# A one-core encoder block: Fourier parts prepared in the attention, a sum made by the fetching DMA, and a merge in program order

## The chip, the cores and the metric

The kernel runs on one core of a Trainium2 chip. The metric is the device time of one execution in microseconds (us). The kernel before took 1730.04 us (median of 3 runs, 1729.23 to 1732.54).

## The reference, cut to what matters

One encoder layer is run on two sequences, 256 and 1024 positions, each with 16 meta tokens ahead, at width 1024, all in float32:

```python
h = rms_norm(x, norm_mix_g)
z = h @ w_in          # q | k | v | f | attention gate | Fourier gate
a  = bidirectional_gqa(q, k, v) @ w_attn_o       # 8 query heads, 2 kv heads of 64
fo = fourier_mix(f) @ w_four_o                   # real part of a 2-D DFT, 4 groups of 128
merged = sigmoid(z_attn) * a + sigmoid(z_four) * fo
x = x + merged @ w_out
u = rms_norm(x, norm_ffn_g) @ w_ffn_in
x = x + (silu(gate) * up) @ w_ffn_out            # d_ff 2816, then a final rms_norm
```

## The kernel before, in words

Every float32 product is made of float32r parts. An operand is cast on ScalarE to a high part, and the rest is subtracted into a low part on VectorE or GpSimd (`split`, line 204). TensorE then adds three products, high by high, high by low and low by high (`three`, lines 224 to 226). Tokens are cut into chunks 0 and 1 (512 sample tokens each) and 2 (256 prompt tokens).

SBUF is a set of 48 slots of 128 x 1056 elements (27 single ones, 7 triples), handed out in the order in which they came free (`Slots`). Whoever gets a slot waits, on the chip, until its former users are through with it.

The stages, in order: norm and Fourier input (`stage_a`); the DFT (`fourier`), whose result goes folded to DRAM as `f_d`, 516 rows by 656 columns; `q_pass` and `kv_pass`; the attention; the merge; `w_out`; the two feed-forward products. The gate logits (`gate_gen`) are 16 units of 128 rows. Each is a product for each chunk, stored to DRAM (`gates`). They fill gaps of TensorE: in the attention the loop calls `gates(FILL[kind])` after every step, and the filler issues product groups until their costs (640 for a group of three 512-column matmuls, 320 for 256 columns) have used up what was added.

The attention takes ten tiles of 128 queries, the two prompt tiles first, each in two groups of four heads. A head is a score product (L891) into the one score buffer, a maximum (L896), an exponential (L903), and a scaling. A second part follows one group later: transposes (L825), a cast and a subtraction (L827, L828), and products with the values (L845, L846). The last group's second part is the drain. The result of a group is written to DRAM, twice: as both value parts' products, `a_d[c][0]` and `a_d[c][1]`, whose sum is the attention's output.

Inside a `manual_schedule` block TensorE, ScalarE and VectorE execute in the order in which the program names their work. Outside, and for SyncE and GpSimd always, a planner orders each engine's instructions by dependencies and estimated times, so a load can be issued well ahead of its place in the program. Each engine works off its own queue in order. The attention is such a block; the merge is not.

After the attention, `fourier_parts` (line 931) fetches `f_d` and splits it into six slots, and the row of channel 64 with its weights into small zero-padded tiles (L947 to L968). `load_af(c)` (line 972) fetches both halves of a chunk of `a_d` (L987), adds them on VectorE (L998) and splits the sum. Chunk 0 is done beside the remaining gates, chunks 2 and 1 after them.

`merge` (line 1003) runs eight steps, one for each 128 rows of the output. `load(i)` fetches three weight pieces (L1015 to L1018) and six gate pieces (L1024) on SyncE's queue. `need(i)` prepares the weights `wf` (Fourier) and `wm` (attention) (L1032 to L1037). `sigmoid(i)` is one activation for each chunk over both gates (L1046). `fourier(i)` makes the Fourier product in four PSUM banks, unfolds it (L1070 to L1078) and multiplies it by its gate on GpSimd (L1087). Then follow the attention products of chunks 0, 2 and 1, each with a gate product (L1125), a sum on GpSimd (L1126), and the rounding of the merged rows into two parts (L1128, L1129). `fourier(i + 1)` is named ahead of step i's attention products. Last, `w_out` loads its weights with `need` (line 1146), a unit ahead of use.

## Time and profile before

| | us |
|---|---|
| median of 3 runs | 1730.04 (1729.23 to 1732.54) |
| the profiled execution: its own time | 1730.22 |
| its span, first to last instruction | 1728.5 |
| TensorE busy in the span | 1679.2 |
| VectorE, ScalarE, GpSimd busy | 1115.0, 720.5, 272.6 |

The times in the views are microseconds from the span's start. PE is TensorE's matmul, PEld its weight load, DVE VectorE, ACT ScalarE, POOL GpSimd, SP SyncE, and SPq its queue of transfers. A number behind L is a line of the kernel. An idle time is put down to what ended it (the releaser); where a wait was for several things, to the last. The granted clock is the share of TensorE's full speed in that stretch.

### The profile page before, as it was taken

The numbers are of one execution on the slowest core, as the hardware profiler recorded it, in microseconds if no ns is written. First come the engines' busy times: TensorE is split into PE (matmuls) and PEld (weight loads), VectorE is DVE, ScalarE is ACT, GpSimd is POOL, SyncE is SP. The second block draws the span as 40 slices with busy tenths as digits, with TensorE's granted clock in tenths as the row PEclk, the third lists the DMA queues.
The fourth block names the chain that finished last, engine by engine and source line by source line (L and its number), as shares of the span: only waits on it lengthen the run. The fifth ranks groups of instructions, "written<-read, shape, count | busy, mean of one in ns | idle before, by whom it ended". The sixth has DMA issues, their size and how long they took to land.

```text
span 1728.5 us, 25882 instructions
## 1 busy us (share of the span) xinstructions
PE 1679.2 (97%) x9837; PEld 1499.2 (87%) x9837; DVE 1115.0 (65%) x2082; ACT 720.5 (42%) x1411; POOL 272.6 (16%) x307
## 2 busy tenths in 40 slices
PE   7999999999999998989989999999999999999997
PEld 7888879878888886878879999999999998888886
DVE  5423544567777775752479676667666768765685
ACT  6323323456666665631355222222222234444444
POOL 3002333210100113663353000000000000000002
PEclk9999999999999998999999999999999999999999
DMA  5144331322212228624442222322232137653534
GB/s 191 57 147 138 116 116 56 122 74 67 70 57 64 62 66 291 212 92 154 162 155 82 87 68 91 102 91 83 95 103 90 65 123 259 199 186 95 162 97 153
DMA packets 97564, 203.03 MB, mean 117 GB/s; under 512 B 10173, under 2 KB 46169, under 8 KB 97440
## 3 DMA queue, kind: packets, MB, share of 16 engines
q1 hardware_dynamic: 88224, 184.22, 32.5%
q10 hardware_dynamic: 7824, 12.53, 2.0%
q0 software_dynamic: 1392, 4.63, 0.9%
q8 instruction: 77, 1.26, 0.3%
q14 instruction: 47, 0.39, 0.1%
HBM read 143.30 MB, written 58.04 MB: 116 GB/s over the span
## 4 chain that ended last, share of the span: by engine, by line
PE 88%; DVE 5%; issue 2%; ACT 2%; POOL 2%; DMA 1%; SPq 0%; POOLq 0%; ACTq 0%; DVEq 0%
PE i L224 10%; PE i L226 10%; PE i L225 10%; PE o L226 5%; PE o L225 5%; PE o L224 5%; PE g L224 4%; PE pt L825 4%; PE g L226 4%; PE S L891 4%; PE g L225 4%; PE pv L845 2%; PE pv L846 2%; PE wo L226 2%; PE wo L225 2%
## 5 line engine op out<-in xcount | busy, mean ns | idle before, releaser
L1320 ACT CAST w<-wi 128x512 fp32r<-128x512 f32 x168 | 104.0, 621 | 273.2 <-PE i L226 223.9
L224 PE MATMUL i<-A,w 128*128 128x384 f32 x616 | 208.6, 339 | 3.0 <-ACT w L1320 2.6
L226 PE MATMUL i<-A,w 128*128 128x384 f32 x616 | 208.3, 339 | 2.4 <-POOL w L1322 2.4
L225 PE MATMUL i<-A,w 128*128 128x384 f32 x616 | 208.1, 338 | 0.0
L226 PE MATMUL i<-Ah,w 128*128 128x256 f32 x616 | 173.3, 282 | 0.0
L224 PE MATMUL i<-Ah,w 128*128 128x256 f32 x616 | 173.1, 281 | 0.2 <-ACT w L1320 0.2
L225 PE MATMUL i<-Al,w 128*128 128x256 f32 x616 | 173.1, 281 | 0.0
L828 DVE TENSOR_TENSOR pT<-pt,pT 128x512 fp32r<-128x512 f32 x156 | 106.9, 686 | 37.9 <-ACT pT L827 36.7
L827 ACT CAST pT<-pt 128x512 fp32r<-128x512 f32 x156 | 90.8, 582 | 95.0 <-PE pt L825 92.1
L1322 DVE TENSOR_TENSOR w<-wi,w 128x512 fp32r<-128x512 f32 x154 | 105.1, 684 | 29.1 <-ACT w L1320 28.6
L233 POOL TENSOR_SCALAR fin0r<-fin0ss 128x1 f32<-128x1 f32 x1 | 0.8, 788 | 755.3 <-ACT X L241 755.3
L224 PEld LDWEIGHTS i<-A,w 128*128 128x128 f32 x616 | 116.5, 189 | 3.5 <-ACT w L1320 2.8
L896 DVE TENSOR_REDUCE sm<-S 128x1 f32<-128x1040 f32 (+1 forms) x80 | 86.5, 1081 | 50.7 <-PE S L891 47.4
L226 PEld LDWEIGHTS i<-A,w 128*128 128x128 f32 x616 | 116.4, 189 | 3.2 <-POOL w L1322 3.2
L224 PEld LDWEIGHTS i<-Ah,w 128*128 128x128 f32 x616 | 116.1, 188 | 0.6 <-ACT w L1320 0.6
L225 PEld LDWEIGHTS i<-A,w 128*128 128x128 f32 x616 | 116.3, 189 | 0.0
L225 PEld LDWEIGHTS i<-Al,w 128*128 128x128 f32 x616 | 116.3, 189 | 0.0
L226 PEld LDWEIGHTS i<-Ah,w 128*128 128x128 f32 x616 | 116.1, 189 | 0.0
L903 ACT ACTIVATE p<-S,sm 128x1040 f32<-128x1040 f32 (+1 forms) x80 | 80.3, 1003 | 33.7 <-DVE sm L896 27.1
L825 PE MATMUL pt<-ident,p 128*128 128x128 f32 (+1 forms) x624 | 93.4, 272 | 0.0
L226 PE MATMUL o<-wfo,act 128*128 128x512 f32 (+1 forms) x212 | 82.1, 388 | 2.0 <-DVE act L1454 2.0
L225 PE MATMUL o<-wfo,act 128*128 128x512 f32 (+1 forms) x212 | 82.0, 387 | 0.0
(747 smaller groups left out, 4438.4 us busy)
## 6 DMA issues: line engine op xcount, KB each, us to landing
wi<-w_fi SPq DMA_DIRECT2D x48, 512.0 KB, 3.5
wg<-w_g SPq DMA_DIRECT2D x32, 512.0 KB, 3.6
act_d<-sc SPq DMA_DIRECT2D x77, 192.0 KB, 1.9
act<-act_d SPq DMA_DIRECT2D x37, 320.0 KB, 4.1
wfo<-w_fo SPq DMA_DIRECT2D x21, 512.0 KB, 4.1
X<-act_d SPq DMA_DIRECT2D x31, 320.0 KB, 3.4
act_d<-sc SPq DMA_DIRECT2D x77, 128.0 KB, 2.3
gate<-gs ACTq DMA_DIRECT2D x32, 256.0 KB, 3.2
```

The source lines that it names most:

```text
L224: mm(out, sh, mh, start=first and i == 0, stop=False)
L225: mm(out, sh, ml, start=False, stop=False)
L226: mm(out, slo, mh, start=False, stop=last and i == n - 1)
L825: nc.tensor.transpose(pt[:rows, h * P : (h + 1) * P], me.ps4[h][:, col : col + rows], self.ident[:])
L827: nc.scalar.copy(pT[:rows, :512], pt[:rows, :])
L828: nc.vector.tensor_tensor(pT[:rows, 512:1024], pt[:rows, :], f32(pT[:rows, :512]), op=ALU.subtract)
L845: nc.tensor.matmul(me.pv[:], vst, pT[:rows, :512], start=j == 0, stop=False)
L891: nc.tensor.matmul(S[:, base + lo : base + hi], hq, self.kT[seq][g][v][:, lo:hi], start=v == 0, stop=v == 1)
L896: nc.vector.tensor_reduce(nb, S[:, base : base + L], axis=AX.X, op=ALU.max, negate=True)
L903: self.last_exp = nc.scalar.activation(p, S[:, base : base + L], AF.Exp, bias=nb, accum_out=total)
L1320: nc.scalar.copy(w[:, :512], src)
L1322: eng.tensor_tensor(w[:, 512:1024], src, f32(w[:, :512]), op=ALU.subtract)
```

## The change

- `fourier_parts` is now stepped inside the attention, once after each head from the loop's step 101 on (tile 4 of the sample), 21 steps in all. Its slots are taken one by one. The subtractions are on GpSimd instead of VectorE. Two slots of prompt keys are given back when the prompt tiles are done.
- `load_af` fetches the first half of a on SyncE's queue and the second on GpSimd's queue with an accumulating DMA into the same tile. The VectorE addition is gone. Chunks 0 and 2 are asked for at the drain's start, chunk 1 after the attention; chunk 0 is split beside the gates, chunk 2 behind them, chunk 1 behind Fourier unit 1 in the merge.
- The filler gets 610 instead of 640 for each step of the sample's attention, and 2600 at five places after it.
- The merge is a manual block. `load` and `load_gates` are two functions. Weights of step i + 3 are asked for, and those of step i + 2 prepared, after step i's first attention product; the gates of step i + 3 after step i, those of step 7 in step 5. `sigmoid` is one activation for each chunk and gate. The rounding of merged rows is put off by one product (`late`).
- `w_out`'s first weight unit is loaded at one call and split at the next.

```diff
+PARTS = 100
...
-    FILL = {"s": 640, "p": 400, "end": 640, "drain": 900}
+    FILL = {"s": 610, "p": 400, "end": 640, "drain": 900}
...
                 sl.put(q.pop(t))
+                if t == 9:
+                    sl.put(*self.kv_slots[4:6])
                 if t == tiles[-1]:
-                    sl.put(*self.kv_slots[:6])
+                    sl.put(*self.kv_slots[:4])
...
+        slots = self.fparts = {}
+
+        def block(i):
+            if i // 3 not in slots:
+                slots[i // 3] = sl.get("fx", F32R, "t")
+            return slots[i // 3][:, i % 3 * HL : (i % 3 + 1) * HL]
+
+        self.fblock = block
+        block(17)
+        y = self.y64 = sl.get("y64", F32R, "t")
+        tails = [(slots[5][:, HL : 3 * HL], self.f_d[512:516, :], NL, 32), (y[:, :D], a["w_64"], D, 64)]
+        raw = [sl.get("x64r") for _ in tails]
+        for r, (t, src, n, _) in zip(raw, tails):
+            nc.gpsimd.memset(f32(t[:68, :]), 0.0)
             for b in (0, 32, 64):
...
-        self.fblock = lambda i: slots[i // 3][:, i % 3 * HL : (i % 3 + 1) * HL]
+        yield 1
+        yield 1
+        for r, (t, _, n, lo) in zip(raw, tails):
+            for b in (0, 32, 64):
+                nc.scalar.copy(t[b : b + 4, :], r[b : b + 4, :n])
+            x = slice(lo, lo + 4)
+            nc.gpsimd.tensor_tensor(t[x, :], r[x, :n], f32(t[x, :]), op=ALU.subtract)
+            sl.put(r)
+            yield 1
         for k in range(4):
-            r = raw.pop(k)
+            r = sl.get("fr")
+            nc.sync.dma_start(r[:, :NL], self.f_d[k * P : (k + 1) * P, :])
+            yield 1
+            yield 1
             for half in range(2):
                 src = r[:, half * HL : (half + 1) * HL]
-                h, l = self.fblock(4 * k + 2 * half), self.fblock(4 * k + 2 * half + 1)
+                h, l = block(4 * k + 2 * half), block(4 * k + 2 * half + 1)
                 nc.scalar.copy(h, src)
-                nc.vector.tensor_tensor(l, src, f32(h), op=ALU.subtract)
+                nc.gpsimd.tensor_tensor(l, src, f32(h), op=ALU.subtract)
+                yield 1
             sl.put(r)
...
         def load(i):
-            if i == len(pieces):
-                return
-            srcs, j = pieces[i]
-            loaded[i] = [sl.get("af") for _ in srcs]
-            for src, raw in zip(srcs, loaded[i]):
-                nc.sync.dma_start(
...
+            if i < 4 // per:
+                raws[i] = sl.get("af")
+                for x, queue in enumerate((nc.sync, nc.gpsimd)):
+                    src = self.a_d[c][x][i * per * P : (i + 1) * per * P, :].rearrange("(k p) n -> p k n", p=P)
+                    queue.dma_start(raws[i].v(per, n), src, **({"accum_op": ALU.add} if x else {}))
 
         load(0)
+        load(1)
         yield 1
-        for i in range(len(pieces)):
-            load(i + 1)
-            raws = loaded.pop(i)
-            if len(raws) == 2:
-                r, x = (r[:, :1024] for r in raws)
-                nc.vector.tensor_tensor(r, r, x, op=ALU.add)
-            out.append(self.split(raws[0], 1024, "af", nc.vector, "t"))
-            sl.put(*raws)
+        for i in range(4 // per):
+            raw = raws.pop(i)
+            out.append(self.split(raw, 1024, "af", nc.vector, "t"))
+            sl.put(raw)
...
             r = sl.get("wmf")
             nc.sync.dma_start(r[:, :512], a["w_mf"][i])
@@ -1017,6 +1015,10 @@
             q = sl.get("wma")
             nc.sync.dma_start(q[:, :512], a["w_ma"][i])
             raws[i] = r, q
+
+        def load_gates(i):
+            if i >= 8:
+                return
             g = gts[i] = [sl.get("gt") for _ in range(3)]
...
+        def sigmoid(i, which):
             for c in range(3):
-                g = gts[i][c][:, : 2 * CH_N[c]]
+                n = CH_N[c]
+                g = gts[i][c][:, which * n : (which + 1) * n]
                 with self.tc.issue_after(self.last_exp.ins):
                     nc.scalar.activation(g, g, AF.Sigmoid)
...
             w = wf.pop(i)
+            sigmoid(i, 0)
             for half in range(2):
...
                     pp.append(pm)
+                while late:
+                    late.popleft()()
                 st = sl.get("fst")
                 nc.scalar.copy(st[:, :HL], pp[0][:, :HL])
...
         load(0)
+        load_gates(0)
         yield 0
         need(0)
         load(1)
+        load_gates(1)
         for c in range(3):
             self.M[c] = [], []
-        sigmoid(0)
+        yield 0
+        need(1)
+        load(2)
+        load_gates(2)
         yield from fourier(0)
-        need(1)
-        sigmoid(1)
-        load(2)
         for i in range(8):
             yield from fourier(i + 1)
+            if i == 0:
+                run_all(self.last_af)
+            if i == 5:
+                load_gates(7)
             if i == 6:
-                sl.put(*self.fparts, self.y64)
+                sl.put(*self.fparts.values(), self.y64)
             if i == 7:
                 next(then)
+            sigmoid(i, 1)
...
                     mv = tuple(af[c][k // per][x][:, (k % per) * n : (k % per + 1) * n] for x in range(2))
                     self.three(pm[:, :n], [(wk, mv)], k == 0, k == 3)
                     yield 3 * n / 2.4
+                if c == 0:
+                    need(i + 2)
+                    load(i + 3)
                 v = gt[:, n : 2 * n]
                 nc.vector.tensor_tensor(v, pm[:, :n], v, op=ALU.mult)
                 nc.gpsimd.tensor_tensor(v, v, gt[:, :n], op=ALU.add)
-                b = (i % per) * n
-                nc.scalar.copy(mh[-1][:, b : b + n], v)
-                nc.vector.tensor_tensor(ml[-1][:, b : b + n], v, f32(mh[-1][:, b : b + n]), op=ALU.subtract)
-                sl.put(gt)
-                if c == 2 and i < 6:
-                    need(i + 2)
-                    sigmoid(i + 2)
+                while late:
+                    late.popleft()()
+
+                def rows(gt=gt, v=v, b=(i % per) * n, n=n, h=mh[-1], l=ml[-1]):
+
+                    nc.scalar.copy(h[:, b : b + n], v)
+                    nc.vector.tensor_tensor(l[:, b : b + n], v, f32(h[:, b : b + n]), op=ALU.subtract)
+                    sl.put(gt)
+
+                late.append(rows)
+                if c == 2 and i == 7:
+                    next(then)
             sl.put(w)
-            if i < 5:
-                load(i + 3)
+            if i < 4:
+                load_gates(i + 3)
+        while late:
+            late.popleft()()
         for c in range(3):
...
-        need(0)
+        raw = sl.get("wo", F32, "s")
+        nc.sync.dma_start(raw[:, :1024], a["w_out"][0])
+        yield 0
+        units[0] = self.split(raw, 1024, "wo", nc.gpsimd, "s")
+        sl.put(raw)
         yield 0
...
                 if i == 7:
                     next(then)
+                    next(then, None)
...
-                for kind, more, slack in self.attention(ps, [8, 9] + list(range(8)), "S", "pv"):
+                parts = self.fourier_parts()
+                for i, (kind, more, slack) in enumerate(self.attention(ps, [8, 9] + list(range(8)), "S", "pv")):
                     while slack and later:
                         later.popleft()()
+                    if slack and i > PARTS:
+                        next(parts, None)
+                    if kind == "drain" and not self.af:
+                        next(m)
+                        early = chain(self.load_af(0), self.load_af(2))
+                        next(early)
                     gates(self.FILL[kind] + more)
                 while later:
                     later.popleft()()
                 self.later = None
-            early = chain(self.fourier_parts(), self.load_af(0))
-            next(early)
-            next(m)
-            for _ in early:
-                gates(1300)
-            gates.rest()
+                run_all(parts)
+                gates(2600)
+                next(m)
+                self.last_af = self.load_af(1)
+                for i, _ in enumerate(early):
+                    gates(2600)
+                    if i == 0:
+                        next(self.last_af)
+                gates.rest()
             self.free_hT(self.hT[1])
...
-            for c in (2, 1):
-                run_all(self.load_af(c))
...
-            run_all(m)
+            with self.tc.manual_schedule(engines={E.PE, E.Activation, E.DVE}):
+                run_all(m)
```

36 lines of the change are left out of this document (4 added, 32 removed).

## The prediction

> **What bounds the kernel now.** First the page's span and engine shares, then the windows by stage (columns: stretch, its length, busy time of PE, its weight loads, DVE, ACT and POOL, granted clock, DMA share, GB/s).
>
> ```profile
> span 1728.5 us, 25882 instructions
> PE 1679.2 (97%) x9837; PEld 1499.2 (87%) x9837; DVE 1115.0 (65%) x2082; ACT 720.5 (42%) x1411; POOL 272.6 (16%) x307
> ...
> 400.00:640.00 240.00, 240.00 (x1478) 206.03 (x1477) 189.79 (x284) 153.06 (x278) 23.79 (x19) 1.00 0.21 61
> 640.00:659.90 19.90, 19.90 (x119) 16.19 (x117) 10.75 (x18) 14.73 (x25) 5.73 (x5) 1.00 0.57 170
> 659.90:667.70 7.80, 7.80 (x46) 6.87 (x46) 0.00 (x0) 5.38 (x7) 1.87 (x1) 1.00 0.69 173
> 667.70:680.00 12.30, 6.69 (x36) 5.21 (x34) 9.99 (x15) 5.83 (x11) 3.83 (x3) 0.99 1.05 387
> 680.00:693.00 13.00, 9.86 (x26) 6.80 (x27) 10.96 (x13) 4.64 (x7) 7.89 (x7) 0.50 1.03 369
> 693.00:753.10 60.10, 59.49 (x340) 53.88 (x339) 43.15 (x85) 34.12 (x56) 39.51 (x50) 1.00 0.52 176
> 753.10:768.00 14.90, 9.96 (x52) 8.79 (x51) 8.82 (x19) 3.89 (x8) 10.34 (x17) 0.89 0.17 56
> ```
>
> TensorE is busy 97% of the span, so only its own idle and slow time can be won. The attention (to 659.9) and the gates after it leave none. The merge starts at 667.7, and there the idle time is 12.30-6.69 = 5.61, 13.00-9.86 = 3.14, 60.10-59.49 = 0.61 and 14.90-9.96 = 4.94: 14.30 us. The clock adds to it: at 0.50 the 9.86 us of work of 680 to 693 would take 4.93, so 4.93 are lost, and 0.11 x 14.90 = 1.64 in the last window. What the merge can give is 14.30+6.57 = 20.9 us. Next the waits of PE there (total, times, longest), and the timeline of PE at the two long ones and at one whole chunk.
>
> ```profile
> PE fo L224 <- ACT wm L1036: 7.6, 2, 4.5
> PE m L224 <- ACT afh L208: 2.0, 2, 1.5
> PE m L225 <- DVE afh L209: 1.8, 1, 1.8
> ```
> ```profile
> 671.15 0.42 PE L224 MATMUL fo<-fx,wm 128*128 128x328 f32 x1 [3.10 <-ACT wm L1036]
> ...
> 720.65 0.32 PE L1059 MATMUL fo<-fx,y 68*128 68x328 f32 x1
> ...
> 724.54 0.40 PE L224 MATMUL m<-y,ml 128*128 128x512 f32 x1
> ...
> 731.46 0.31 PE L1059 MATMUL fo<-fx,y 68*128 68x328 f32 x1
> ...
> 757.88 0.42 PE L224 MATMUL fo<-fx,wm 128*128 128x328 f32 x1 [4.47 <-ACT wm L1036]
> ```
>
> A Fourier unit takes 724.54-720.65 = 3.9 us of PE, a step with its three attention products 731.46-720.65 = 10.8; the products' 6.9 split by their 512, 256 and 512 columns into 2.76, 1.38 and 2.76. The start (to 693.7) waits for weights, then for the halves of a: 9.36 us idle and 4.93 of clock, 14.3. The second place, 753.1 to 768, waits once more for weights: 4.94 and 1.64, 6.6. Why they are late stands in the chain of waits, in the DMA issues (KB each, median us to landing) and in SyncE's timeline and waits.
>
> ```profile
> 660.89 0.32 SPq L855
> ...
> 664.17 7.98 DMA af<-a_d
> 672.25 1.24 DVE af L998
> ```
> ```profile
> wi<-w_fi SPq DMA_DIRECT2D x48, 512.0 KB, 3.5
> af<-a_d SPq DMA_DIRECT2D x10, 512.0 KB, 6.8
> a_d<-ao SPq DMA_DIRECT2D x36, 128.0 KB, 2.5
> tabc<-pos_c POOLq DMA_DIRECT2D x4, 520.0 KB, 4.9
> ```
> ```profile
> 729.22 13.38 SPq L1024 DMA_DIRECT2D gt<-gate  x10
> 746.99 0.33 SPq L1015 DMA_DIRECT2D wmf<-w_mf  x1
> ```
> ```profile
> SPq L1015 <- DVE wmf L1032: 9.8, 1, 9.8
> ```
>
> At the start ten fetches of a, the last two of the map and three sets of weights and gates ask at once; the DMA engines are full (387 and 369 GB/s), and the five DVE additions follow. At 753 the weights were asked for at 746.99, behind ten gate fetches that took 13.38 us to be issued.
>
> **The change part by part.**
>
> *Second place.* Weights of step 7 are asked for after the first product of step 4, no longer behind gate fetches. The products at 724.54 are step 3's, so that is 724.54+2.76+10.8, some 738, against 746.99; they are split after the first product of step 5, 10.8 us later, and a load of that kind lands in 3.5 to 6.8. By my count of the allocator 44 of 48 slots are then taken, so SyncE need not wait long. Value taken: the whole 6.6 is won; bounds 0 (the old slot wait of 9.8 comes back) and 6.6. The gates of step 7 are now asked for late, in step 5; what is late next is ScalarE's sigmoid of step 6, and PE can run through 3.9+6.9 us of work on its eight PSUM banks before it needs that.
>
> *Start: what goes.* The map's four 128-row pieces and their small rows are prepared in the attention: eight 128x328 casts and eight subtractions leave the start. The five additions leave DVE. Fetches of chunks 0 and 2 of a, and weights and gates of step 0, are asked for in the drain (640 to 659.9, where DMA is at 0.57) and just after. FILL 610 for 640 holds back 120 x 30 = 3,600 of gate work by the program's costs. The 7.80 us from 659.9 hold seven groups costed 640 and eight costed 320, 7,040, so 3,600 are 4.0 us of PE, out of the attention and into the gap. PE time is only moved; but the gates then last 7.8+4.0 = 11.8 us after the attention, and with Fourier unit 0 (3.9, its weights split early) PE has work for 15.7 us.
>
> *Start: what comes.* PE, ACT and DVE now keep program order. The split of chunk 2 of a stands on ACT and DVE ahead of the weights of Fourier unit 1. So unit 1 waits for three accumulating fetches on POOL's queue (two of chunk 1, one of chunk 2), each behind its plain fetch. No trace row shows an accumulating fetch. The last stores of a go out 1.0 us after the attention (660.89), land in 2.5; with their issue about 4.4. Plain fetch: 3.5 (alone) to 6.8 (in the crowd), to 7.9 or 11.2. Accumulate: near bound 4.9, the POOL-queue load of its size, one after the other sharing the engines at 387 GB/s (0.5 MB is 1.4 us): the third lands at 7.9+4.9+1.4 = 14.2 to 11.2+4.9+2.7 = 18.8. Far bound twice 6.8, since it must read and write its target: 11.2+13.6+2.7 = 27.5. Then the split and the weights:
>
> ```profile
> 673.51 1.05 ACT L208 CAST y<-af 128x1024 fp32r<-128x1024 f32 x1 [0.20 <-DVE af L998]
> L209 DVE TENSOR_TENSOR afl<-af,afh 128x1024 fp32r<-128x1024 f32 x2 | 2.5, 1226 | 0.1
> 690.74 0.41 DVE L1032 TENSOR_TENSOR wmf<-wmf 128x256 f32<-128x256 f32 x1
> 691.80 0.61 ACT L1036 CAST wm<-wmf 128x512 fp32r<-128x512 f32 x1
> ```
>
> 1.05+1.23+2 x 0.41+0.61 = 3.7. Unit 1 can start at 17.9 to 22.5 (31.2 at the far bound), PE is there at 15.7: a wait of 2.2 to 6.8 (15.5), or none if chunk 2, whose store is old, is fetched first. I take 5.0, nearer the rows of loads than the doubled one. Chunk 1's own splits (2 x 1.05+1.23 = 3.3) come behind unit 1 and lie under two products, 4.1 us: 0.
>
> A wait of that length costs clock: after the 4.47 us wait 1.64 were lost; I take 1.6, bounds 0 and 4.9. Here the Trainium skill is to be weighed (TensorE: Matmul & The Clock Gate, section "Why this matters for your kernels"): it wants no idle gaps above about 3 us and holds that shorter ones keep the clock. The trace shows 0.50 after a row of waits of which none but the first, 3.10, passed 1.8. By the rule, waits in short pieces would cost nothing and the sum would be 1.6 lower; by the trace it could be 3.3 higher. The measurement decides.
>
> *Attention.* What is added there must fit ScalarE. Timeline rows and groups:
>
> ```profile
> 650.40 2.11 ACT L966 CAST y<-y64r 4x1024 fp32r<-4x1024 f32 x2
> 653.64 0.74 ACT L966 CAST fx<-x64r 4x656 fp32r<-4x656 f32 x1
> 620.69 1.11 PE L891 MATMUL S<-kT,qT 128*128 128x264 f32 x6
> 624.82 1.11 PE L891 MATMUL S<-kT,qT 128*128 128x264 f32 x6
> L896 DVE TENSOR_REDUCE sm<-S 128x1 f32<-128x1040 f32 x53 | 65.8, 1242 | 24.4 <-PE S L891 24.4
> L903 ACT ACTIVATE p<-S,sm 128x1040 f32<-128x1040 f32 x54 | 61.2, 1133 | 11.1 <-DVE sm L896 11.1
> L1087 POOL TENSOR_TENSOR gt<-fst,gt 128x328 f32<-128x328 f32 x8 | 8.9, 1113 | 25.2 <-DMA af<-a_d 12.8 <-DMA wmf<-w_mb 6.6 <-DVE fst L1077 5.7
> ```
>
> A head comes every 624.82-620.69 = 4.13 us; scores, maximum and exponential, 1.11+1.24+1.13 = 3.48, run in series on the one score buffer, so 0.65 is spare. ACT is busy 153 of 240, leaving 1.5 per head. The three 4x1024 copies (3.15) come in one head: 3.15-1.5-0.65 = 1.0 us late. The three of 0.74 (2.2) and the single casts fit. Value 1.0, bounds 0 and 5.4 (both bursts whole). POOL's eight subtractions at about 1.1 lie in its idle time (23.8 of 240 busy). Slots are nearly all in use then (47 of 48 by my count), but each comes back from PE work that precedes the next use in order: 0, covered by that order; if it fails, each of some 28 heads with the map's slots out loses what its wait has above the 0.65, and 1 us each would be 28.
>
> *End of the merge.* The first split of w_out follows the second product of step 7; its low part is POOL's.
>
> ```profile
> L209 POOL TENSOR_TENSOR wol<-wo,woh 128x1024 fp32r<-128x1024 f32 x14 | 34.6, 2480 | 41.2 <-ACT woh L208 36.0 <-PE wo L226 4.4 <-DVE ml L1129 0.7
> ```
>
> These 2.48 us, behind 1.05 of cast, have the third product (2.76) and the first high matmuls to lie under: 0.5 us, bounds 0 and 2.5.
>
> *Sum.* The profiled execution took 1730.2 (span 1728.5 and 1.7 around it), as the median of 1730.04. -20.9+5.0+1.6+1.0+0.5 = -12.8: 1717.4 us. From 1712 to 1722 I call this case mine.
>
> **The rivals.**
>
> *All hidden.* The planner still orders SyncE and POOL and may send weights and chunk 2 ahead of chunk 1, as it sent step 0's weights into the drain before; then nothing waits: 1730.2-20.9+1.5 = 1710.8. Against it: the last stores bound chunk 1, and some megabytes must still come.
>
> *Order costs in each step.* Rows wait on ACT for POOL's sum, in order, and hold up the copies behind them, which free PSUM. POOL was busy 39.51 of 60.10, so it has room, and rows come one product late; but the planner's own order lost only 0.61 us in 60. If a step loses 1 us, eight lose 8 on top of mine: 1725.4. About there too (1725.1) lies the case in which DMA is as full as before, the start keeps its 14.3 and only the second place goes.
>
> *The accumulating fetch is slow: slower than before.* It is one mechanism at the start. If the three run one after the other at X us each from 11.2 on, unit 1 starts at 14.9+3X, PE waits 3X-0.8, and with 1.6 of clock and 1.5 elsewhere the gain of 20.9 is eaten at X = 6.2 (85 GB/s). At 8.5: 24.7+1.6+1.5-20.9 = +6.9, 1737.1. For it: nothing bounds X from above but the guess of doubling, and POOL's queue waits in order. Against it: a plain load on that queue lands as fast as on the others.
>
> **How the numbers follow.** Mine 0.42, all hidden 0.20, the cases near 1725 0.15, those costs together eating the gain 0.10, slow accumulate 0.13. Changes under 0.2% (3.5 us) can't be told from none. Faster: 0.42+0.20+0.15 = 0.77; same 0.10; slower 0.13. The range runs from 1708 (all hidden, and the 1.5 elsewhere won too) to 1730; outside stay the slow accumulate and about 0.03 below.
>
> **What would show it.** No wait on weights above 1 us in steps 1 to 7, and the clock at 1.00 there: second place right. One wait of Fourier unit 1 of 2 to 7 us, its releaser DVE or ACT behind chunk 2's split, the accumulating fetches landing in 5 to 7 us: the start right; no wait there, or one over 10, makes me wrong on either side. Score matmuls of the later tiles waiting for ACT by 1 us in all: the attention right; several us in many heads would show the slots or POOL instead. Waits of PE on PSUM in each step would show the order's cost.

## The result: 12 us slower

| | before | after |
|---|---|---|
| median of 4 runs, us | 1729.96 (1729.23 to 1732.54) | 1742.17 (1741.58 to 1744.49) |
| ratio, 95% interval | | 1.0070 (1.0053 to 1.0088) |
| span of the profiled execution | 1728.5 | 1740.3 |

The forecast was 1717.4, in a range of 1708 to 1730. The result lies above it: 12.2 us longer than before, where 12.8 less was forecast.

### The profile page after: what moved, and what is told of

It is laid out like the page before. It is cut to its first block, busy times and chain, and to the rows that moved or that the text cites. A ratio compares the mean times of both kernels' runs of the same rounds, so it can differ in the third digit from the quotient of the medians.

```text
span 1740.3 us, 25889 instructions
## 1 busy us (share of the span) xinstructions
PE 1680.9 (97%) x9837; PEld 1498.8 (86%) x9837; DVE 1102.5 (63%) x2069; ACT 722.9 (42%) x1435; POOL 278.3 (16%) x320
## 4 chain that ended last, share of the span: by engine, by line
PE 84%; DVE 5%; ACT 3%; DMA 3%; POOL 3%; issue 3%; SPq 0%; POOLq 0%; ACTq 0%; DVEq 0%
PE i L227 10%; PE i L225 10%; PE i L226 10%; PE o L227 5%; PE o L225 5%; PE o L226 5%; PE g L225 4%; PE S L892 4%; PE g L227 4%; PE g L226 4%; PE pt L826 4%; PE pv L846 2%; PE pv L847 2%; PE wo L226 1%; PE wo L227 1%
## 5 line engine op out<-in xcount | busy, mean ns | idle before, releaser
L829 DVE TENSOR_TENSOR pT<-pt,pT 128x512 fp32r<-128x512 f32 (+1 forms) x138 | 94.6, 686 | 36.6 <-ACT pT L828 34.8
L828 ACT CAST pT<-pt 128x512 fp32r<-128x512 f32 (+1 forms) x138 | 80.3, 582 | 85.2 <-PE pt L826 80.9
L227 PE MATMUL o<-wfo,act 128*128 128x512 f32 (+1 forms) x212 | 82.1, 388 | 1.6 <-DVE act L1480 1.6
L826 PEld LDWEIGHTS pt<-ident,p 128*128 128x128 f32 (+1 forms) x624 | 72.6, 134 | 11.1 <-issue 0.3
```

Of the source, the lines that this page charges most:

```text
L227: mm(out, slo, mh, start=False, stop=last and i == n - 1)
L826: nc.tensor.transpose(pt[:rows, h * P : (h + 1) * P], me.ps4[h][:, col : col + rows], self.ident[:])
L828: nc.scalar.copy(pT[:rows, :512], pt[:rows, :])
L829: nc.vector.tensor_tensor(pT[:rows, 512:1024], pt[:rows, :], f32(pT[:rows, :512]), op=ALU.subtract)
```

## The profile after

First the page's head, then PE's waits between 655 and 800 us (total, times, longest).

```profile
span 1740.3 us, 25889 instructions
PE 1680.9 (97%) x9837; PEld 1498.8 (86%) x9837; DVE 1102.5 (63%) x2069; ACT 722.9 (42%) x1435; POOL 278.3 (16%) x320
```
```profile
PE fo L1061 <- ACT fst L1074: 15.3, 1, 15.3
PE fo L225 <- ACT wm L1038: 2.8, 4, 0.7
PE wo L226 <- POOL wol L210: 2.3, 1, 2.3
PE wo L225 <- ACT woh L209: 1.7, 1, 1.7
PE fo L227 <- DVE wm L1039: 0.8, 5, 0.2
```

The wait of 4.5 us on the weights of step 7 is gone. In its place stand one wait of 15.3, a small one in every step, and two at the end of the merge. PE's timeline gives the marks by which the loss can be placed: the first matmul of Fourier units 0, 1, 4 and 7, the last one of the merge, the first two of `w_out`, the first of the feed-forward product.

```profile
673.13 0.32 PE L1061 MATMUL fo<-fx 68*128 68x328 f32 x1
...
692.51 0.64 PE L1061 MATMUL fo<-fx 68*128 68x328 f32 x1 [15.31 <-ACT fst L1074]
...
727.80 0.31 PE L1061 MATMUL fo<-fx 68*128 68x328 f32 x1
...
764.70 0.31 PE L1061 MATMUL fo<-fx 68*128 68x328 f32 x1
...
783.70 0.40 PE L227 MATMUL m<-wm,wm 128*128 128x512 f32 x1
785.77 0.50 PE L225 MATMUL wo<-woh,afl 128*128 128x512 f32 x1 [1.68 <-ACT woh L209]
788.55 0.51 PE L226 MATMUL wo<-wol,afl 128*128 128x512 f32 x1 [2.27 <-POOL wol L210]
...
906.98 0.34 PE L225 MATMUL i<-A,w 128*128 128x384 f32 x1
```

| stretch, from mark to mark | before | after | difference |
|---|---|---|---|
| start to Fourier unit 0 (attention and gates) | 667.73 | 673.13 | +5.40 |
| unit 0 to unit 4 (start of the merge) | 52.92 | 54.67 | +1.75 |
| unit 4 to unit 7 (three steps) | 32.46 | 36.90 | +4.44 |
| unit 7 to first `wo` matmul | 24.46 | 21.07 | -3.39 |
| first `wo` matmul to feed-forward | 117.68 | 121.21 | +3.53 |
| sum | 895.25 | 906.98 | +11.73 |

The sum is the whole difference of the spans (11.8): nothing moved behind 907. So the loss has four places and the gain one, and each was tried, the end of the merge only on top of other edits.

## The experiments

### The start: the third chunk is asked for last

The chain of waits at the start, and ScalarE's timeline where it ends:

```profile
663.10 4.34 DMA a_d<-ao
667.46 6.92 DMA af<-a_d
...
674.91 15.31 DMA af<-a_d
```
```profile
690.25 1.04 ACT L209 CAST afh<-af 128x1024 fp32r<-128x1024 f32 x1 [16.77 <-DMA af<-a_d]
...
692.02 0.43 ACT L1074 COPY fst<-fo 128x328 f32<-128x328 f32 x1 [0.45 <-ACT gs L457]
```

The third chunk (chunk 2, the prompt) is asked for last by the program itself. The change is described above as asking for chunks 0 and 2 at the drain's start, but `chain` begins its second generator only when the first has ended, so the fetches of chunk 2 are named behind the attention, behind the splits of chunk 0 and the fetches of chunk 1. Its plain half lands at 674.4, the half that is added to it at 690.2. ScalarE keeps program order, and its copy of unit 0's accumulator, which frees the PSUM bank that unit 1 wants, is named behind the split of that chunk. Unit 1's weights had been ready since 671. Two runs take the mechanism apart: one asks for the chunk early, one lets the second half overwrite instead of add, which leaves the sum out.

```diff
-                        early = chain(self.load_af(0), self.load_af(2))
-                        next(early)
+                        third = self.load_af(2)
+                        next(third)
+                        first = self.load_af(0)
+                        next(first)
+                        early = chain(first, third)
```

> The third chunk of the attention's result, 1 MB in two halves, is asked for ahead of the first one in the attention's drain, some 40 us earlier than in the changed kernel. Theory (the 15.3 us wait of Fourier unit 1 is there because the third chunk's adding fetch is asked for last): ScalarE's wait of 16.77 us ahead of the third chunk's split is below 2 us, the wait on the copy of the Fourier accumulator is below 4 us, and the time falls by 10 to 13 us, to 1729 to 1732. Rival (the fetches of these 20 us together, 8.4 MB at 240 to 275 GB/s until about 690, set the end whatever their order): the wait moves to the first chunk or to the weights and 8 us or more of it stay, 1736 to 1742.

Measured: 1728.15 us, 0.9986 (0.9976 to 0.9995). The wait of unit 1 is gone; units 0 and 1 adjoin (672.69 and 676.60). The theory holds, and the gain of 14 us is more than the 10 to 13 expected. Chunk 1's two adding fetches are now the last, issued from 673.0 on; ScalarE splits what they bring at 682.7 and 686.4, and two matmuls wait for the second split, for 1.0 and 0.8.

```diff
-                    queue.dma_start(raws[i].v(per, n), src, **({"accum_op": ALU.add} if x else {}))
+                    queue.dma_start(raws[i].v(per, n), src)
```

> The second half of each chunk is fetched by the same queue into the same place at the same time, but written instead of added; so the sum of the two halves is left out of the computation. Theory (adding is what makes these fetches slow, 176 GB/s in service): the landing of the third chunk's second half falls from 15.3 us to 6 to 8, the wait of Fourier unit 1 from 15.3 to 7 or less, and the time by 7 to 9 us, to 1733 to 1735. Rival (the DMA engines are full of all that is fetched there, and adding costs nothing by itself): landing 12 us or more, 1740 to 1742.

Measured: 1734.32, 1.0023 (1.0014 to 1.0033); unit 1's wait is 8.3 us, where 7 or less was expected. The bytes, the queue and the order are the same, and the landing of the third chunk's second half falls from 15.3 to 8.7, where 6 to 8 was expected. The DMA page of the two kernels between 600 and 720 us (packets, MB, share of 16 engines) and the tile's DMA groups (ns, min, median, max) show why:

```profile
q0 software_dynamic: 1616, 2.62, 12.8%
```
```profile
L990 POOL DMA_DIRECT2D af<-a_d x5: 1194/1201/1537, 624.7 to 674.9; - x5
...
DMA to landing us min/median/max: 6.7/9.7/15.3
```

and with the second half written:

```profile
q0 software_dynamic: 720, 2.62, 6.1%
```
```profile
L990 POOL DMA_DIRECT2D af<-a_d x5: 722/727/815, 623.4 to 673.2; - x5
...
DMA to landing us min/median/max: 4.3/7.9/8.7
```

Adding takes 2.1 times the engines' time for the same 2.62 MB. So of unit 1's 15.3 us about 7 are the adding itself; the other 8 stay with plain writes and come from asking last in a full stretch, since asking early removes them too. Asked for early, the adding leaves no wait at unit 1.

### The attention: two bursts of small copies

ScalarE's timeline in the attention, and PE's waits there, 2.7 us in all:

```profile
521.13 2.26 ACT L959 CAST fx<-x64r 4x656 fp32r<-4x656 f32 x3
524.38 1.13 ACT L904 ACTIVATE p<-S,sm 128x1040 f32<-128x1040 f32 x1 [0.38 <-POOL fx L961]
...
526.49 3.19 ACT L959 CAST fx<-x64r 4x1024 fp32r<-4x1024 f32 x3
530.31 1.13 ACT L904 ACTIVATE p<-S,sm 128x1040 f32<-128x1040 f32 x1
```
```profile
PE S L892 <- ACT p L904: 2.7, 2, 2.2
```

The bursts come in neighbouring heads. One copy to a head instead:

```diff
                 nc.scalar.copy(t[b : b + 4, :], r[b : b + 4, :n])
+                yield 1
```

> The six copies of the two 4-row tails into the Fourier parts, three in a burst in each of two heads, go one to a head. Theory (the bursts of 2.26 and 3.19 us on ScalarE delay two exponentials, and they are most of the 5.4 us that the attention lost): the two waits of 0.50 and 2.20 us of the score matmuls at 525 to 532 us go, the last pv matmul comes 3 to 5 us earlier than 661.85, and the time falls by 3 to 5 us, to 1737 to 1739. Rival (the attention loses a little in every head, to all 24 preparing instructions and the longer gate work, not to the bursts): the last pv matmul moves by less than 1.5 us, 1741 to 1742.

Measured: 1725.22, 0.9978 (0.9967 to 0.9988), 17 us less than the changed kernel where 3 to 5 were expected. The attention does what was expected: its waits fall to 0.2 and its last matmul comes at 656.64, 4.8 us earlier. The rest came unasked. The planner still orders SyncE's and GpSimd's queues, and with six more steps of parts it put the third chunk's fetch ahead of chunk 1's; why it did is not shown. The first row below is of SyncE after the change, where all three fetches stand together. The second is of this run, where one has come forward to 649.95. It is the third chunk's, as its split, the third in ScalarE's order, now starts at 667.9.

```profile
664.71 3.10 SPq L990 DMA_DIRECT2D af<-a_d  x3
```
```profile
649.95 0.42 SPq L991 DMA_DIRECT2D af<-a_d  x1
```

Unit 1's wait is then 1.5 us. So this run undoes the start's loss as well, by the cause that the run with the early third chunk had shown, and its 17 us must not be booked on the bursts. By unit 0's mark in all profiles: five of the before kind stand at 667.6 to 668.2 (mean 667.9), five with the bursts at 671.8 to 673.1 (672.4), seven with the copies spread at 668.4 to 670.6 (669.8). The bursts cost about 2.6 us, and about 1.9 us of the loss up to unit 0 stay with the spread copies. What these are was not settled.

### The steps: a closed trip of 12.3 us

After the start every step takes 12.30 us, with PE at work for 11.4 of it and the clock full. Windows (stretch, length, PE busy, granted clock, DMA share, GB/s), and one step on ScalarE, VectorE and GpSimd:

```profile
729.80:742.10 12.30, 11.44 (x64) 1.00 0.53 172
742.10:754.40 12.30, 11.41 (x64) 1.00 0.30 86
```
```profile
740.41 0.62 ACT L1038 CAST wm<-wmf 128x512 fp32r<-128x512 f32 x1 [1.97 <-DVE wmf L1035]
...
744.62 0.62 ACT L1146 CAST wm<-gt 128x512 fp32r<-128x512 f32 x1 [3.07 <-POOL gt L1140]
...
748.08 0.62 ACT L1146 CAST mh<-gt 128x512 fp32r<-128x512 f32 x1 [1.00 <-POOL gt L1140]
748.61 0.76 ACT L1074 COPY fst<-fo 128x328 f32<-128x328 f32 x2
...
752.73 0.62 ACT L1038 CAST wm<-wmf 128x512 fp32r<-128x512 f32 x1 [2.01 <-PE m L227]
```
```profile
741.67 0.89 DVE L1039 TENSOR_TENSOR wm<-wma,wm 128x512 fp32r<-128x512 f32 x1
742.48 1.01 DVE L1139 TENSOR_TENSOR gt<-m,gt 128x512 f32<-128x512 f32 x2
...
745.88 0.69 DVE L1139 TENSOR_TENSOR gt<-m,gt 128x512 f32<-128x512 f32 x1
...
751.47 0.47 DVE L1034 TENSOR_TENSOR wmf<-wmf 128x256 f32<-128x256 f32 x1
751.86 0.80 DVE L1035 TENSOR_TENSOR wmf<-wmf 128x256 f32<-128x256 f32 x1
```
```profile
743.30 1.98 POOL L1140 TENSOR_TENSOR gt<-gt 128x512 f32<-128x512 f32 x2 [1.29 <-DVE gt L1139]
746.65 1.40 POOL L1140 TENSOR_TENSOR gt<-gt 128x512 f32<-128x512 f32 x1 [1.36 <-DVE gt L1139]
```

Read in order of time this is a ring. ScalarE copies the weights (740.41), VectorE subtracts (to 742.5) and only then multiplies the chunk's product by its gate, GpSimd adds (743.30), ScalarE rounds the row (744.62), VectorE multiplies the next product (745.88), GpSimd adds (746.65), ScalarE rounds (748.08) and now copies the Fourier accumulator (748.61), VectorE forms the Fourier sums and then the weights' additions (751.47), for which ScalarE's next copy (752.73) has waited. Its row names PE, but by the rows PE's matmul ended at 752.52 and the additions at 752.66, and the row a round before names the additions. 752.73-740.41 = 12.3. No engine is full; PE waits once a round for each of the two parts of the weights, 0.7 and 0.2 us. First, the order given back to the planner:

```diff
-            with self.tc.manual_schedule(engines={E.PE, E.Activation, E.DVE}):
-                run_all(m)
+            run_all(m)
```

> The merge's steps are ordered by the planner again, as before the change; everything else of the change stays (parts in the attention, accumulating fetch, rows one chunk late, weights asked for early). Theory (a fixed program order makes one closed trip ACT, DVE, POOL, ACT of 12.3 us in each step): the distance of the first matmuls of Fourier units 4 and 7 falls from 36.9 us to about 32.5 (3 x 10.83), and the time by 5 to 7 us, to 1735 to 1737. Rival (the trip lies in the work itself, rows one chunk late and split sigmoids, and no order shortens it): 36.9 us stays and 1742. Second rival (the order also causes the wait of Fourier unit 1, since the copy of its accumulator stands in a fixed place behind the third chunk's split): the 15.3 us shrink as well, to 5 or less, and the time is 1728 or less.

Measured: 1732.66, 1.0016 (1.0006 to 1.0025). Units 4 to 7 are 32.75 us apart, and the wait of unit 1 stays at 15.1. That is the theory and not the second rival: the third chunk's split stands in the attention's block, whose order is still fixed. The time is 2 us less than the theory gave: from unit 7 to the first `wo` matmul it is 17.88 instead of 21.07, since in the planner's order `w_out` also follows directly on the merge's last matmul (777.66 and 777.89). Then the order alone, put on the kernel before (the same two lines the other way):

> The kernel before with the program order alone: the merge's steps on TensorE, ScalarE and VectorE in the order of the program instead of the planner's, nothing else changed. Theory (a fixed order costs in each step by itself, and rows one chunk late only soften it): units 4 and 7, 32.5 us apart in the kernel before, are 37 us apart or more, the wait at the second place may go, and the time is 1735 or more. Rival (the fixed order and the late rows cost only together): 33 us or less apart, 1722 to 1730.

Measured: 1759.89, 1.0174 (1.0159 to 1.0190). Units 4 to 7 are 45.6 us apart, 15.2 for a step. PE's waits there:

```profile
PE fo L224 <- ACT wm L1036: 27.5, 6, 12.0
PE fo L224 <- ACT ml L1036: 5.7, 2, 3.0
```

So the order costs by itself, and what else the change brought to the merge took two thirds of that away again (12.3 for 15.2, where PE needs 10.9). To open the ring without the planner, the weights' preparation was moved behind the first product, together with the spread copies and the early third chunk:

```diff
-                if c == 0:
-                    need(i + 2)
-                    load(i + 3)
                 v = gt[:, n : 2 * n]
...
                 while late:
                     late.popleft()()
+                if c == 0:
+                    need(i + 2)
+                    load(i + 3)
```

> Three edits on the changed kernel: the third chunk asked for first, the tails' copies one to a head (both as in the runs before), and in the merge's fixed order the preparation of the weights two steps ahead (two additions, two copies, two subtractions) moved behind the first chunk's product instead of ahead of it. Theory (what closes the trip of 12.3 us is that ScalarE's copies of the weights wait for VectorE's additions, which stand behind the Fourier sums, and the product of the first chunk stands behind them both): with the product first the trip loses about 3 us, TensorE sets the step again, units 4 to 7 of the Fourier part start 32.5 to 33 us apart instead of 36.9, and the time is 1714 to 1718, from 1725.2 with the spread tails less 6 x 1.45. Rival (any fixed order with the rows one chunk late makes a trip of 12 us): 36 to 37 us stays and 1722 to 1726. Second rival: the weights now come too late for the next unit, the wait on them grows from 0.7 us to 2 or more in each step, and the time is above 1727.

Measured: 1719.03, 0.9936 (0.9921 to 0.9951). Units 4 to 7 are 34.24 us apart, so 11.4 for a step, 60% of the way to the planner's order; 32.5 to 33 was expected, and the time is 1 us above the expected 1714 to 1718. Two additions on VectorE were still in the ring. The next run takes them out; it leaves out the early third chunk and has `w_out` earlier (both below).

```diff
+        def adds(i):
+            if i >= 8:
+                return
+            r, vec = raws[i][0], nc.vector.tensor_tensor
+            vec(r[:, :256], r[:, :256], r[:, 512:768], op=ALU.add)
+            vec(r[:, 256:512], r[:, 768:1024], r[:, 256:512], op=ALU.subtract)
...
         for i in range(8):
+            adds(i + 2)
             yield from fourier(i + 1)
```

> As the run without the early third chunk, and in each step VectorE's two additions for the weights two steps ahead stand at the start of the step, ahead of the Fourier sums; copies and subtractions stay behind the first product. Theory (what is left of the trip, 11.4 us in a step against 10.9 in the planner's order, still holds the additions, 1.27 us on VectorE): the starts of units 4 and 7 are 32.5 to 33 us apart instead of 34.2, and the time is 2 to 4 us less. Rival (the trip is now closed elsewhere, by rows and products, or the weights' subtractions come late for the next unit): 34 us stays, less than 1 us.

Measured: 1711.67, 0.9895 (0.9873 to 0.9916), 4.3 us less than without, though its four runs spread from 1708.8 to 1716.1, and the intervals of the two versions overlap. The profile is of the slowest of the four. Two starts of units, and PE's only wait between 655 and 800 us:

```profile
713.72 0.31 PE L1067 MATMUL fo<-fx 68*128 68x328 f32 x1
...
746.31 0.32 PE L1067 MATMUL fo<-fx 68*128 68x328 f32 x1
```
```profile
PE fo L1067 <- ACT fst L1080: 4.6, 1, 4.6
```

32.59 us: the fixed order now costs nothing in a step. The wait of 4.6 us that is left at unit 1 has another cause than the third chunk: ScalarE's queue, which also issues the gates' stores, stood until 676.5 for a store that was issued at 669.04 and took 7.47 us to land, and the sigmoids and the copy came behind it. The same two moves on the changed kernel, and nothing else:

> The changed kernel with the two edits to the trip alone: VectorE's additions for the weights at the start of a step, copies and subtractions behind the first product. Theory (the steps' loss is this trip's and independent of the attention and the start): the starts of units 4 and 7 are 32.6 us apart instead of 36.9, the wait of Fourier unit 1 stays at 15 us, and the time falls by 6 to 7 us, to 1735 to 1736.5. Rival (with the start late the steps' gain is taken up elsewhere, at the end of the merge): 1738 or more.

Measured: 1731.92, 1.0011 (1.0001 to 1.0020), 10 us less than the changed kernel, more than was expected. Units 4 to 7 are 32.75 apart and unit 1's wait is 14.5, as the theory has it. The surplus is at the marks around: unit 0 comes 1.3 earlier, units 0 to 4 take 1.8 less, and the merge's last matmul adjoins `w_out`'s first (775.07 and 775.30).

### The second place: a wait for a place

The forecast booked 6.6 us here and saw the cause in weights asked for too late. That part alone on the kernel before:

```diff
                 if c == 2 and i < 6:
                     need(i + 2)
+                    load(i + 3)
                     sigmoid(i + 2)
             sl.put(w)
             if i < 5:
-                load(i + 3)
+                load_gates(i + 3)
```

> The kernel before with one part of the change alone: each step's weights are asked for right behind the preparation that frees their place, and no longer with the gates of that step. Theory (the wait of 4.47 us on the weights of step 7 and the half clock behind it come from the weights being asked for with the gates): both go, and the time is 1723 to 1725. Rival (the weights wait for their place on the same queue in any case, and earlier asking moves nothing): the wait stays within 1 us and the time within 1 us of before.

Measured: 1732.21, 1.0013 (1.0004 to 1.0023): nothing is gained. The fetch was issued at 742.57 instead of 746.99, and the copy did not move. SyncE's and ScalarE's rows of this run, and ScalarE's of the kernel before:

```profile
742.57 0.33 SPq L1015 DMA_DIRECT2D wmf<-w_mf  x1
```
```profile
757.50 0.62 ACT L1038 CAST wm<-wmf 128x512 fp32r<-128x512 f32 x1 [1.24 <-POOL gt L1089]
```
```profile
757.21 0.62 ACT L1036 CAST wm<-wmf 128x512 fp32r<-128x512 f32 x1 [1.98 <-POOL gt L1087]
```

The releaser is GpSimd, not a fetch. Two candidates were left: rows that ScalarE must round first, or the place into which it copies. The rows one product late, alone on the kernel before (the change's `late` queue):

```diff
+                while late:
+                    late.popleft()()
+                def rows(gt=gt, v=v, b=(i % per) * n, n=n, h=mh[-1], l=ml[-1]):
...
+                late.append(rows)
```

> The kernel before with another part alone: each chunk's rows are rounded one product late, the planner still orders the merge. The weights asked for early had landed 4 us sooner and left the wait of 4.5 us as it was: ScalarE's copy of them at 757.2 was released by GpSimd's products. Theory (the copy stands behind rows and Fourier copies that wait for GpSimd's sums, and rows one chunk late take that wait from ScalarE): the wait falls below 1 us, units 6 and 7 start 11 us apart with both halves adjoining, and the time is 1723 to 1726. Rival (the copy waits for its own place, which GpSimd's products of the unit before still hold, and the rows are not in its way): the wait stays 3 us or more and the time is 1728 to 1732.

Measured: 1730.64, 1.0002 (0.9992 to 1.0011); the longest wait is 4.1 us. The rival holds. In the kernel before, the allocator hands the Fourier weights of step 7 the slot that unit 6's Fourier sums have just given back, with three other slots free, and GpSimd's products read these sums until 757.2:

```profile
755.17 2.01 POOL L1087 TENSOR_TENSOR gt<-fst,gt 128x7 f32<-128x7 f32 x5 [0.93 <-DVE fst L1077]
```

In the changed kernel it hands them the slot of older weights, last read by TensorE. So the last run exchanges two slots on the kernel before:

```diff
-            for src, out in ((r, wf), (q, wm)):
+            for src, out in ((q, wm), (r, wf)) if i == 7 else ((r, wf), (q, wm)):
```

> The kernel before with one exchange: the two sets of weights of step 7 take each other's places, so the Fourier weights get the place of unit 6's Fourier weights, last read by TensorE near 746, and the attention weights, which are wanted some 10 us later, the place of unit 6's Fourier sums, which GpSimd's products read until 757.2. Fetches, order and amount of work stay as they are. Theory (the wait of 4.5 us at the second place is for a place, and neither for the fetch nor for the rows): the wait falls below 1 us, units 6 and 7 start 11 us apart with their halves adjoining, and the time falls by 4 to 6.6 us, to 1723.5 to 1726. Rival (the queue of ScalarE is what is late there, whatever the place): the wait stays above 3 us, 1728 to 1731. Second rival: the attention weights now come too late for the products of step 7, the wait moves there, within 2 us of before.

Measured: 1724.34, 0.9962 (0.9948 to 0.9976). PE's waits between 700 and 770 us are now this one line:

```profile
PE fo L226 <- DVE wm L1037: 0.8, 2, 0.6
```

ScalarE's copies of the two sets show that the wait went with the place: the Fourier weights now wait for VectorE's additions, and the attention weights, in the place of the Fourier sums, for GpSimd.

```profile
752.78 0.62 ACT L1036 CAST wm<-wmf 128x512 fp32r<-128x512 f32 x1 [1.72 <-DVE wmf L1033]
...
757.14 0.62 ACT L1036 CAST wm<-wma 128x512 fp32r<-128x512 f32 x1 [1.79 <-POOL gt L1087]
```

One line wins 6.5 us (4.2 to 9.0), what the forecast had booked on early weights. The changed kernel won it too, through a different sequence of slots, which nobody had planned.

### The end of the merge, and the parts together

> The three single edits together: third chunk asked for first, tails' copies one to a head, merge's steps ordered by the planner. Theory (three separate losses: attention 5, start 14, steps 6 to 9): first Fourier matmul at 668, no wait above 2 us at the start, units 4 to 7 32.5 to 33 us apart, time 1715 to 1718. Rival (the losses cover one another, as the third chunk comes early already with the spread tails): 1719 to 1724.

Measured: 1722.28, 0.9951 (0.9935 to 0.9968). In the planner's order unit 1 still waited 6.8 us on the copy of the accumulator, against 2 in the fixed order with the same fetches, so 1718 was missed. For the end, `w_out`'s first unit was asked for in step 6 and split at the start of step 7:

```diff
             if i == 6:
                 sl.put(*self.fparts.values(), self.y64)
+                next(then)
...
-                if c == 2 and i == 7:
-                    next(then)
```

> As the run with the three edits together, and the first unit of the output weights asked for one step of the merge earlier and split ahead of the last step's products instead of between them. Theory (the waits on its two parts at the end of the merge, 2.3 and 1.7 us, and the half rate of the next nine matmuls are there because the split stands late): no wait on them above 0.5 us, the last m matmul and the first wo matmul adjoin as in the kernel before, and the time is 2 to 5 us less than without it. Rival (the planner moves the split where it likes, or the slots for it come free no earlier): less than 1 us.

Measured: 1720.04, 0.9942 (0.9927 to 0.9957): 2.2 us less, but a wait of 1.9 on the low part stays. The time is as expected, the waits are not.

> As the run with the weights' preparation behind the first chunk's product, in the fixed order, and the first unit of the output weights asked for one step earlier and split ahead of the last step's products. Theory: the gap between the last m and the first wo matmul (1.7 us) and the one behind the first wo matmul (2.3 us) go, with the slow matmuls behind them, 4 to 6 us less than without, 1709 to 1714. Rival (the split delays the last step's sigmoids on ScalarE and the wait only changes its name): less than 1.5 us.

Measured: 1717.51, 0.9927 (0.9912 to 0.9942), 1.5 us less than without, where 4 to 6 were expected. The gap ahead of the first `wo` matmul, one of the two that should go, was gone without this edit already (763.67 and 763.91). From the first `wo` matmul to the feed-forward product it is 117.27 us instead of 119.60, so the other wait is indeed gone (0.5 is left); but this run's merge ended 1.2 us later.

> As the fastest run so far (tails one to a head, third chunk asked for first, weights' preparation behind the first product, output weights a step earlier), but the third chunk is asked for in its place in the changed kernel. With the spread tails alone the first Fourier matmul stood at 668.35 and unit 1's wait was 1.5 us; with the third chunk first as well it stands at 669.9 to 670.6. Theory (the third chunk asked for early gives nothing more once the tails are spread, and costs the attention's drain 1.5 to 2 us): first Fourier matmul at 668.4, time 1715 to 1716.5. Rival (the later start is chance of the slots, and without the early third chunk unit 1 waits): 1717.5 or more.

Measured: 1715.97, 0.9921 (0.9905 to 0.9937). The time is in the theory's range, but not by the theory: in the profile, which is of the slowest of the four runs (1719.21), unit 0 stands at 669.97, hardly earlier than with the early third chunk (670.59), and unit 1 waits 3.9. The intervals of these two versions overlap, so once the tails are spread these runs don't show whether the early third chunk gains or costs anything.

The fastest version is the one with the opened ring, 1711.67: the change, with copies of the tails one to a head, the weights' additions at the start of a step and the rest of their preparation behind the first product, and `w_out` one step earlier. It beats both kernels, and the one before by 1.05% (0.84 to 1.27).

## Why the prediction was wrong, step by step

| term of the sum | forecast | measured | by |
|---|---|---|---|
| start: wait of unit 1 | 5.0 (0 to 15.5) | 15.3 | row of PE, early third chunk |
| its clock | 1.6 | 1.7 | 14 matmuls at 0.27 for 0.15 |
| attention | 1.0 (0 to 5.4) | 5.4, 4.5 by the means | marks, spread copies |
| order in each step | 0 (rival: 1 a step) | 1.45 a step | order given back, ring opened |
| second place | -6.6 | -6.2 to -6.5 | exchanged slots |
| end of the merge | 0.5 (0 to 2.5) | 5.4 | 1.84 ahead of the first `wo` matmul, 3.53 behind |

The four terms that failed, 10.3 + 4.4 + 4.4 + 4.9 = 24.0 us by the table (the order over three steps), are nearly the whole of the 25.0 between the forecast (12.8 less) and the result (12.2 more).

*Start: what goes* was right: the preparation left the start, and the old 14.3 went with it. *Start: what comes* named the right mechanism, a wait behind the third chunk's split, and failed in its size. It put the last landing at 14.2 to 18.8 us after the attention and the far bound at 27.5; counted from the end of the last product with the values, near 661.9, it was 28.4. The plain half was late already (12.5 instead of 7.9 to 11.2), and the price of adding was taken from a plain load's landing, 4.9, though the doubled price was written beside it. Doubling was right for the engines' time: 12.8% for 6.1%. The value was chosen nearer the rows that existed, which were rows of another operation. The prediction also said that nothing would wait if the third chunk were fetched first; that sentence was the cure, and in the run with the spread tails the planner did it unasked. But it listed chunk 2's fetches among those asked for in the drain and just after, while the program names them behind chunk 1's; its sum, all the same, took them as the last. And the waiting instruction was not the one named: not the weights, but the copy that frees a PSUM bank, which stood behind the same split. The rival of the slow accumulating fetch came nearest at the start and still fell short: by its formula a last landing at 28.4 is 11.2 + 3 x 5.7, and it needed 6.2 for a loss from the start alone.

*Attention.* The bursts were seen, and the spare time of a head was set against each of them by itself; the smaller one was said to fit. They came in two neighbouring heads, and both delayed an exponential. That the upper bound of 5.4 is the measured sum is chance, as only about half of it is the bursts'.

*Order costs in each step* was a rival, rightly described (rows wait for GpSimd in order and hold up the copies behind them) and thought small because GpSimd had room and the planner's own steps lost next to nothing. Room on each engine says nothing of a ring: at 12.3 us none of the four was full. The planner's 0.61 us in 60 showed that the dependencies allow 10.8, not that this order does. The loss also showed as waits for weights, not as the waits on PSUM that the prediction named as its sign. This failure costs 4.4 us in three steps.

*Second place*: the right number, by luck, for a wrong reason: asking earlier gained nothing, and the new sequence of slots happened to give a free place. The fetch at 746.99 and its 9.8 us of waiting on SyncE were read as the cause because they came first in time. The row of ScalarE's copy, released by GpSimd, was not read.

*End of the merge*: the low part's 2.48 us were laid under the third product, but its high part is copied by ScalarE, which runs late in the ring, and the first matmuls behind the waits ran at half rate (0.42 apart for 0.23). The bound of 2.5 left both out.

The clock, where it was weighed: the wait of 15.3 was followed by 4.3 us at about half rate. The steps with waits of 0.7 and 0.2 us kept 1.00, which agrees with the Trainium skill (TensorE: Matmul & The Clock Gate, section "Why this matters for your kernels"). Waits of about 2 us went both ways. In the run with the two edits to the trip, `w_out`'s second matmul waited 2.22 us, and the granted clock was 0.59 from 780 to 783; in the run with the weights' preparation behind the first product it waited 2.23, and the clock stayed at 1.00. What tells the two apart is open. In the changed kernel the clock cost 1.7 us at the start and, with ten intervals between `wo` matmuls taking 3.99 us for 2.3, about as much at the end; the second has no term in the forecast.

## What to carry to other kernels

Where an order is fixed by hand, follow one step around all its engines until the chain returns to its first instruction: the length of that ring is the period, however idle each engine is. Here two moves took 1.4 us off each step without taking any work out. Before a late wait is put down to a late fetch, read who released the waiting instruction; with shared slots it may wait for its place, and any edit ahead of it deals the slots anew. When a chunk that nobody needs yet is split by an engine in program order ahead of a copy that everybody waits for, ask for it first.

## What the runs showed of the hardware

A fetch that adds into its target took 2.24 times the packets (1616 for 720) and 2.1 times the engine time of one that writes the same bytes, and 1.20 us of GpSimd's queue to issue instead of 0.73. In a full stretch it landed in up to 15.3 us for 8.7. Five VectorE additions leave for it. Whether that pays was not measured by itself, as no run keeps the rest of the change and adds on VectorE; with the third chunk asked for early, unit 1 did not wait for it.
